# Column order of the inner MLP products: two halves of a row in turn, and other places for the rows

## The chip, the core and the metric

The kernel runs on one core of a Trainium2 chip. The metric is the time of one execution in microseconds (us), as the device reports it. A core has five instruction streams that matter here: PE (TensorE, matrix products; its weight loads are listed as PEld), DVE (VectorE), ACT (ScalarE), POOL (GpSimd) and SP, whose queue issues most of the DMAs. SBUF is the on-chip memory of 128 partitions that all engines read; PSUM takes the products.

## What is computed

One inference step of a decoder with two layers over 256 prompt tokens and 64 sample tokens, 320 columns in all, at width 2048. Layer 0 mixes tokens with gated linear attention, layer 1 with gMLP spatial gating. Each layer ends with a squared-ReLU MLP of inner width 8192 and two residual LayerNorms:

```
def sq_relu_mlp(x, w1, w2):
    return jnp.square(jax.nn.relu(x @ w1)) @ w2

x = layer_norm(DEEPNORM_ALPHA * x + h, ln1_g[i], ln1_b[i])
x = layer_norm(DEEPNORM_ALPHA * x + sq_relu_mlp(x, mlp_w1[i], mlp_w2[i]), ln2_g[i], ln2_b[i])
```

All inputs are float32. The change touches only the second MLP product, the one with w2.

## The kernel before

**Layout.** Activations lie transposed: features on the 128 partitions, the T = 320 tokens as columns. An activation of 2048 features is a tile of KT = 16 rows of 320 float32 per partition, 1280 bytes a row. `bigtile` allots BIG = 16 x 320 + 64 floats for it and begins the rows LINE // 2 = 32 floats (128 bytes) into the tile; `parts` makes two such tiles, a high and a low part. In the compiled program every one of these tiles begins at a multiple of 256 bytes, and a row is 5 x 256 bytes, so all rows of all high and low parts begin 128 bytes past a multiple of 256. The tile that feeds a fused LayerNorm (`dgh`, `dgl`) has rows of TW = 322 columns from offset 0: its row k begins 8k bytes past a multiple of 256.

**Products.** A float32 product is made of three products in the type float32r, each a matmul with 128 x 128 weights and 320 moving columns: low weights by high activations, high weights by low activations, high by high (`mm3`, lines 158 to 163). The three add into one PSUM bank. This document calls one such set a triple.

**Weights.** `unit` brings 512 rows by 256 columns of a weight matrix: one DMA of 512 KB from SP's queue, a cast on ACT for the high part `wh` (line 144), a subtraction on DVE for the low part `wl` (line 145). The parts lie in two rings of four buffers; each `wh` begins at a multiple of 256 bytes and each `wl` 64 bytes past one. `group` makes 256 output columns: four units, and for each unit two 128-column halves by four rows, that is 8 triples or 24 matmuls a unit. `gemm` runs eight groups.

**The MLP.** `mlp` works in four chunks of 2048 inner features. For chunk c, a gemm with w1 makes the chunk: its evictions (`evict`, `sq_relu`) square the ReLU and split it into `hh` (ACT, line 856) and `hl` (DVE, line 857). A gemm with w2 follows, with `hh` and `hl` as moving operands: 8 groups x 4 units x 24 = 768 matmuls, 256 triples. For chunks 0 to 2, `evz` adds each PSUM result to the residual `z` (DVE, line 876); for chunk 3, `residual_gemm` does so and feeds the LayerNorm. There are two layers, so eight such w2 stages; `h_in` names the tile pair, "b" in layer 0 and "a" in layer 1. The order of the instructions on an engine is the order of the calls here; `Side` objects spread other work between units, but none runs in the w2 stages.

Of the kernel before, what the change touches and what calls it, by code (L numbers as in the profile page):

```python
# [9 lines left out]
F32R = mybir.dt.float32r  # L10
# [6 lines left out]
D = 2048  # L17
KT = D // P
TP = 256
DB, DS = 8, 8  # L20
T = TP + DB * DS
# [10 lines left out]
UN = 256  # L32
NU = KT // UK
WARM = 9
LINE = 64
BIG = KT * T + LINE


# [6 lines left out]
class Ring:  # L45
# [5 lines left out]
    def part(self, p, name):  # L51

        t = self.pool.tile([P, UK, UN], F32R, tag=p + self.tag, name=name)
        if not self.gap:
            self.pool.tile([P, LINE // 4], F32, tag="gap", name=name + "_gap", bufs=1)
            self.gap = True
# [21 lines left out]
def step_kernel(ctx: ExitStack, tc: tile.TileContext, A):  # L78
# [3 lines left out]
    def nm(s):  # L82
        uid[0] += 1
        return f"{s}_{uid[0]}"
# [16 lines left out]
    def mmtile(n=T):  # L101

        if mx is not None:
            banks[0] = (banks[0] + 1) % 6
        return (mx if banks[0] > 3 else mm).tile([P, n], F32, tag="mm", name=nm("mm"), padded_shape=[P, 512])
# [16 lines left out]
    nc.vector.memset(eps_h[:], HEAD_EPS)  # L122
    cp.tile([P, LINE - 8], F32, tag="fill", name="fill")

# [4 lines left out]
    def unit(w, row0, q, col0, ring):  # L129

        raw = wraw.tile([P, UK, UN], F32, tag="raw", name=nm("raw"))
        src = w[row0 // (UK * P) + q, col0 // UN]
        hi = ring.part("h", nm("wh"))
        lo = ring.part("l", nm("wl"))
        units[0] += 1
        step = 2 if units[0] <= 2 else UK
        for k in range(0, UK, step):
            nc.sync.dma_start(raw[:, k : k + step, :], src[:, k : k + step, :])
        step = 1 if units[0] == 1 else step
        for k in range(0, UK, step):  # L140
            ks = slice(k, k + step)
            if units[0] == 1:
                before_unit(k)
            nc.scalar.copy(hi[:, ks, :], raw[:, ks, :])  # L144
            nc.vector.tensor_sub(lo[:, ks, :], raw[:, ks, :], hi[:, ks, :].bitcast(F32))  # L145
        return hi, lo
# [7 lines left out]
    def next_ring():  # L154
        turn[0] += 1
        return rings[turn[0] % len(rings)]

    def mm3(ps, wh, wl, kk, n, rh, rl, k, c0, cn, first, last):
        s = slice(n * P, (n + 1) * P)
        x_h, x_l = rh[:, k, c0 : c0 + cn], rl[:, k, c0 : c0 + cn]  # L160
        nc.tensor.matmul(ps, wl[:, kk, s], x_h, start=first, stop=False)  # L161
        nc.tensor.matmul(ps, wh[:, kk, s], x_l, start=False, stop=False)  # L162
        nc.tensor.matmul(ps, wh[:, kk, s], x_h, start=False, stop=last)  # L163

    def group(w, row0, cols, rh, rl, evict, side=None, width=T, before=None):

        ps = [mmtile(width) for _ in range(2 * len(cols))]
        for q in range(NU):
            if before is not None:
                before(q)  # L170
            for i, c in enumerate(cols):
                wh, wl = unit(w, row0, q, c, next_ring())
                for n in range(2):
                    for kk in range(UK):
                        k = q * UK + kk
                        mm3(ps[2 * i + n][:], wh, wl, kk, n, rh, rl, k, 0, width, k == 0, k == KT - 1)
                if side is not None:
                    side()
        for n in range(2 * len(cols)):
            evict(n, ps[n])  # L180
# [14 lines left out]
    w_in = A["gla_w_in"]  # L195
    C_Q, C_K, C_V, C_R = 0, H * DK, 2 * H * DK, 2 * H * DK + H * DV

    def bigtile(tag, dt, name, width=T):

        t = (lp if tag == "b1" else big).tile([P, BIG], dt, tag=tag, name=nm(name))
        start = LINE // 2 if width == T else 0
        return t[:, start : start + KT * width].rearrange("p (k t) -> p k t", t=width)

    def parts(pair, name, width=T):
        return bigtile(pair + "0", F32R, name + "h", width), bigtile(pair + "1", F32R, name + "l", width)

    xh, xl = parts("a", "x")  # L210
    o_all = bigtile("b0", F32, "o_all")
# [21 lines left out]
    def load_x(q):  # L233
        for i, raw in enumerate(x_in(q)):
            x_parts(slice(4 * q + 2 * i, 4 * q + 2 * i + 2), raw[:, :, 0:T])
# [55 lines left out]
    def load_gates():  # L291

        nc.sync.dma_start(wgr, A["gla_w_low"])
        wgr2 = gp.tile([P, 2, DV], F32, tag="vtp", name="wgr2")[:].rearrange("p a b -> p (a b)")
        for i in range(6):
            nc.sync.dma_start(wgr2[16 * i : 16 * (i + 1), :], A["gla_w_gate"])
        nc.scalar.copy(wg2[:], wgr2[0:96])
        nc.vector.tensor_sub(wg2[64:96, :], wgr2[64:96], wg2[64:96, :].bitcast(F32))
# [347 lines left out]
    for h, hd in enumerate(hds):  # L646
        gates = [hd.gate_logits, hd.gate_sums, hd.gate_decays]
        if h == 0:

            side = Side([lambda: None, lambda: load_x(1), lambda: None, lambda: load_x(2), lambda: load_gates(),  # L650
                         lambda: load_x(3), low_gate, *gates], 4 * NU)
# [5 lines left out]
        side = Side(hd.steps(), 2 * NU + (2 * NU if h < H - 1 else 2))  # L657
# [10 lines left out]
    def second_half():  # L668
# [12 lines left out]
        rings.append(Ring(wb, "b"))  # L681
        wb.tile([P, LINE // 4], F32, tag="fill", name="fill_b", bufs=1)
        z = lp.tile([P, KT, T], F32, tag="z", name="z")
        lp.tile([P, 3 * LINE // 4], F32, tag="fill", name="fill_l")
        for q in range(2):
# [112 lines left out]
            nc.vector.tensor_mul(t[:], t[:], self.rstd[:])  # L798
            return t, wgb[:, 1:2]

    def gemm(w, row0, col0, rh, rl, evict, quad=False, side=None, before=None, before_last=None):

        i = 0
        while i < D // UN:
            n2 = 2 if quad and i == 0 else 1
            group(w, row0, [col0 + (i + m) * UN for m in range(n2)], rh, rl,
                  lambda n, ps, i=i: evict(2 * i + n, ps), side, before=before if i == 0 else before_last if i == D // UN - 1 else None)
            i += n2

    def gemm_of(norm, out, w, col0, evict_raw, evict):  # L810
# [7 lines left out]
            group(w, 0, (col0 + i * UN,), yh, yl, lambda n, ps, i=i: evict(2 * i + n, ps))  # L818
        return yh, yl

    def residual_gemm(w, rh, rl, row0, scale, vg, vb, raw, quad=False, side=None, before=None, last=False):

        norm = None

        def evict(j, ps):
            nonlocal norm
            if j == 0:
                norm = Norm(z, vg, vb, raw, last)
            zj = z[:, j, :]
            if j < KT // 2:  # L830
                nc.vector.scalar_tensor_tensor(zj, zj, scale, ps[:], op0=ALU.mult, op1=ALU.add)
            else:
                nc.vector.tensor_add(zj, zj, ps[:])
            norm.add(j)
            if j == KT // 2 - 1:
                for i in range(KT // 2, KT):
                    zi = z[:, i, :]
                    nc.vector.scalar_tensor_tensor(zi, zi, scale, norm.c[:], op0=ALU.mult, op1=ALU.subtract)

        gemm(w, row0, 0, rh, rl, evict, quad, side, before)  # L840
        return norm

    def mlp(i, norm, y_in, h_in, vg, vb, raw, last=False):

        w1, w2 = A["mlp_w1"][i], A["mlp_w2"][i]
        NC_ = 4
        for c in range(NC_):
            hs = []

            def sq_relu(j, x, r):  # L850
                if not hs:
                    hs.extend(parts(h_in, "h"))
                hh, hl = hs
                f = l2.tile([P, T], F32, tag="f", name=nm("f"))
                nc.vector.scalar_tensor_tensor(f[:], x, 0.0, r[:], op0=ALU.max, op1=ALU.mult)
                nc.scalar.copy(hh[:, j, 0:T], f[:])  # L856
                nc.vector.tensor_sub(hl[:, j, 0:T], f[:], hh[:, j, 0:T].bitcast(F32))  # L857

            def evict(j, ps):
                r = l2.tile([P, T], F32, tag="r", name=nm("r"))  # L860
                nc.scalar.activation(r[:], ps[:], AF.Relu)
                sq_relu(j, ps[:], r)

            def evict_raw(j, ps):
                t, wb_ = norm.correct(ps)
                r = l2.tile([P, T], F32, tag="r", name=nm("r"))
                nc.scalar.activation(r[:], t[:], AF.Relu, bias=wb_)
                sq_relu(j, r[:], r)

            if c == 0:  # L870
                yh, yl = gemm_of(norm, y_in, w1, 0, evict_raw, evict)
            else:
                gemm(w1, 0, c * D, yh, yl, evict)
            if c < NC_ - 1:
                def evz(j, ps, s=ALPHA if c == 0 else 1.0):
                    nc.vector.scalar_tensor_tensor(z[:, j, :], z[:, j, :], s, ps[:], op0=ALU.mult, op1=ALU.add)
                gemm(w2, c * D, 0, *hs, evz)
            else:
                return residual_gemm(w2, *hs, c * D, 1.0, vg, vb, raw, last=last)


    def before(q):
        if q == NU - 1:
            second_half()
        else:
            split_o(range(UK * q, UK * (q + 1)))

    norm = residual_gemm(A["gla_w_out"], oh, ol, 0, ALPHA, V_L1G, V_L1B, "b", quad=True,
                         side=side, before=before)
# [87 lines left out]
    side = Side(steps, 6 * NU)  # L977
# [23 lines left out]
    ps = {}  # L1001
# [103 lines left out]
```

## Time and profile before

| what | value |
|---|---|
| median of 3 runs | 2704.8 us (2704.26 to 2705.38) |
| profiled execution, its own time | 2703.75 us |
| span of the profiled execution | 2702.0 us |
| instructions on PE | 18515 matmuls, 18515 weight loads |
| read from HBM | 409.60 MB |

The span runs from the first to the last instruction of the profile; the execution's own time lies 1.75 us above it. [...]

The eight w2 stages lie as follows (first matmul with `hh` or `hl`, us from the span's start; layer 0, then layer 1): 667.1, 889.0, 1110.9, 1332.7; 1907.0, 2128.8, 2350.7, 2572.6. Each is about 110.9 us long. Between them lie the w1 gemms of the same length.

### The profile page before, as it was taken

The numbers are of one execution on the slowest core, as the hardware profiler recorded it, in microseconds if no ns is written. First come the engines' busy times: TensorE is split into PE (matmuls) and PEld (weight loads), VectorE is DVE, ScalarE is ACT, GpSimd is POOL, SyncE is SP. The second block draws the span as 40 slices with busy tenths as digits, with TensorE's granted clock in tenths as the row PEclk, the third lists the DMA queues.
The fourth block names the chain that finished last, engine by engine and source line by source line (L and its number), as shares of the span: only waits on it lengthen the run. The fifth ranks groups of instructions, "written<-read, shape, count | busy, mean of one in ns | idle before, by whom it ended". The sixth has DMA issues, their size and how long they took to land.

```text
span 2702.0 us, 44679 instructions
## 1 busy us (share of the span) xinstructions
PE 2692.4 (100%) x18515; PEld 2669.7 (99%) x18515; DVE 1543.5 (57%) x2289; ACT 1182.8 (44%) x1702; POOL 53.5 (2%) x83
## 2 busy tenths in 40 slices
PE   9999999999999999999999999999999999999998
PEld 9999999999999999999999999999999999999998
DVE  6667577885444444444468775587444444444456
ACT  6545455464234334333445554355334323333434
POOL 1000001000000000000001000000000000000000
PEclk9999999999999999999999999999999999999999
DMA  7656556644445455444445444454444545554442
GB/s 243 193 188 228 185 190 218 211 146 156 152 151 154 151 154 151 153 151 153 150 148 171 150 140 136 140 162 155 150 155 150 154 151 153 152 153 152 153 152 79
DMA packets 126396, 434.53 MB, mean 161 GB/s; under 512 B 13680, under 2 KB 17904, under 8 KB 126192
## 3 DMA queue, kind: packets, MB, share of 16 engines
q1 hardware_dynamic: 119136, 407.82, 48.6%
q0 software_dynamic: 6512, 23.20, 2.6%
q8 instruction: 145, 2.38, 0.4%
q10 hardware_dynamic: 544, 0.66, 0.1%
q14 instruction: 59, 0.48, 0.1%
HBM read 409.60 MB, written 22.02 MB: 160 GB/s over the span
## 4 chain that ended last, share of the span: by engine, by line
PE 99%; ACT 0%; DMA 0%; DVE 0%; issue 0%; ACTq 0%; DVEq 0%
PE mm L161 32%; PE mm L163 31%; PE mm L162 31%; PE gl L600 1%; PE gl L603 1%; PE gl L558 1%; PE gl L948 0%; PE gl L542 0%; DMA raw<-gla_w_in 0%; ACT z L1038 0%; PE gl L943 0%; DMA xr<-xT 0%; PE gl L543 0%; PE gl L458 0%; PE gl L456 0%; PE gl L521 0%
## 5 line engine op out<-in xcount | busy, mean ns | idle before, releaser
L145 DVE TENSOR_TENSOR wl<-raw,wh 128x1024 fp32r<-128x1024 f32 (+1 forms) x740 | 901.6, 1219 | 938.8 <-ACT wh L144 936.3
L144 ACT CAST wh<-raw 128x1024 fp32r<-128x1024 f32 (+1 forms) x740 | 771.3, 1044 | 1201.3 <-PE mm L163 1080.9
L163 PE MATMUL mm<-yh,wh 128*128 128x320 f32 x2624 | 805.0, 307 | 0.0
L161 PE MATMUL mm<-yh,wl 128*128 128x320 f32 x2624 | 803.1, 308 | 0.0
L162 PE MATMUL mm<-yl,wh 128*128 128x320 f32 x2624 | 794.2, 303 | 0.0
L161 PE MATMUL mm<-hh,wl 128*128 128x320 f32 x2048 | 630.8, 308 | 0.0
L163 PE MATMUL mm<-hh,wh 128*128 128x320 f32 x2048 | 628.7, 307 | 0.0
L162 PE MATMUL mm<-hl,wh 128*128 128x320 f32 x2048 | 619.6, 303 | 0.0
L162 PEld LDWEIGHTS mm<-yl,wh 128*128 128x128 f32 x2624 | 492.5, 188 | 0.0
L161 PEld LDWEIGHTS mm<-yh,wl 128*128 128x128 f32 x2624 | 490.9, 188 | 0.0
L163 PEld LDWEIGHTS mm<-yh,wh 128*128 128x128 f32 x2624 | 490.8, 187 | 0.0
L162 PEld LDWEIGHTS mm<-hl,wh 128*128 128x128 f32 x2048 | 384.4, 188 | 0.0
L161 PEld LDWEIGHTS mm<-hh,wl 128*128 128x128 f32 x2048 | 384.4, 188 | 0.0
L163 PEld LDWEIGHTS mm<-hh,wh 128*128 128x128 f32 x2048 | 383.0, 187 | 0.0
L161 PE MATMUL mm<-xh,wl 128*128 128x320 f32 x768 | 241.1, 314 | 0.9 <-DVE wl L145 0.5
L163 PE MATMUL mm<-xh,wh 128*128 128x320 f32 x768 | 236.7, 308 | 0.0
L162 PE MATMUL mm<-xl,wh 128*128 128x320 f32 x768 | 234.7, 306 | 0.0
L161 PEld LDWEIGHTS mm<-xh,wl 128*128 128x128 f32 x768 | 144.1, 188 | 5.4 <-issue 1.9
L162 PEld LDWEIGHTS mm<-xl,wh 128*128 128x128 f32 x768 | 144.3, 188 | 3.5 <-issue 1.2
L163 PEld LDWEIGHTS mm<-xh,wh 128*128 128x128 f32 x768 | 143.9, 187 | 1.3
L857 DVE TENSOR_TENSOR hl<-f,hh 128x320 fp32r<-128x320 f32 x128 | 62.3, 489 | 29.4 <-ACT hh L856 29.4
L161 PE MATMUL mm<-oh,wl 128*128 128x320 f32 x256 | 78.1, 309 | 0.6 <-DVE nw L187 0.6
(268 smaller groups left out, 2112.2 us busy)
## 6 DMA issues: line engine op xcount, KB each, us to landing
raw<-mlp_w SPq DMA_DIRECT2D x512, 512.0 KB, 3.5
raw<-gla_w_in SPq DMA_DIRECT2D x94, 512.0 KB, 4.2
raw<-sg_w_in SPq DMA_DIRECT2D x64, 512.0 KB, 3.5
st<-state SPq DMA_DIRECT2D x32, 512.0 KB, 4.3
o_state_s<-st POOLq DMA_DIRECT2D x32, 512.0 KB, 3.8
raw<-gla_w_out SPq DMA_DIRECT2D x32, 512.0 KB, 4.2
raw<-sg_w_out SPq DMA_DIRECT2D x32, 512.0 KB, 3.5
z<-xT POOLq DMA_DIRECT2D x2, 1280.0 KB, 11.6
```

The costliest lines, as they stand in the source:

```text
L144: nc.scalar.copy(hi[:, ks, :], raw[:, ks, :])
L145: nc.vector.tensor_sub(lo[:, ks, :], raw[:, ks, :], hi[:, ks, :].bitcast(F32))
L161: nc.tensor.matmul(ps, wl[:, kk, s], x_h, start=first, stop=False)
L162: nc.tensor.matmul(ps, wh[:, kk, s], x_l, start=False, stop=False)
L163: nc.tensor.matmul(ps, wh[:, kk, s], x_h, start=False, stop=last)
L558: nc.tensor.matmul(pu[:], hd.ktp[:, blk, kt * P : (kt + 1) * P], hd.vtp[:, blk, :], start=(blk == 0), stop=(blk == 1))
L600: nc.tensor.matmul(po[:], qm[:, kt, b * P : (b + 1) * P], part[:], start=False, stop=(b == DB - 1 and kt == 1 and part is sth))
L603: nc.tensor.matmul(pu[:], kz[:, g, i, kt * P : (kt + 1) * P], hd.vts[:, g, :], start=True, stop=True)
L857: nc.vector.tensor_sub(hl[:, j, 0:T], f[:], hh[:, j, 0:T].bitcast(F32))
```

## The change

A table `TURNS` gives every w2 stage two numbers: the offset in floats at which the rows of `hh` and `hl` begin in their tiles, and a run length. With a run length, `by_turns` views the 320 columns of a matmul's moving operand and of its PSUM output as two halves of 160, and orders them as a run from the first half, the run at the same place of the second half, the next run of the first, and so on. The same columns meet the same PSUM addresses as before; only the order in which they pass is another. Chunk 0 of layer 0 keeps its offset and its plain order.

| stage | layer 0, c=0 | c=1 | c=2 | c=3 | layer 1, c=0 | c=1 | c=2 | c=3 |
|---|---|---|---|---|---|---|---|---|
| offset, floats | 32 | 32 | 32 | 32 | 16 | 0 | 48 | 16 |
| run, floats | none | 4 | 8 | 16 | 4 | 4 | 4 | 8 |

The other lines of the diff pass the two numbers down through `gemm`, `residual_gemm`, `group`, `parts` and `bigtile`.

```
+TURNS = [[(32, None), (32, 4), (32, 8), (32, 16)], [(16, 4), (0, 4), (48, 4), (16, 8)]]
...
-    def mm3(ps, wh, wl, kk, n, rh, rl, k, c0, cn, first, last):
+    def by_turns(ap, run):
+
+        return ap if run is None else ap.rearrange("p (j i e) -> p i j e", j=2, e=run)
+
+    def mm3(ps, wh, wl, kk, n, rh, rl, k, c0, cn, first, last, run):
         s = slice(n * P, (n + 1) * P)
-        x_h, x_l = rh[:, k, c0 : c0 + cn], rl[:, k, c0 : c0 + cn]
+        ps, x_h, x_l = (by_turns(ap, run) for ap in (ps, rh[:, k, c0 : c0 + cn], rl[:, k, c0 : c0 + cn]))
         nc.tensor.matmul(ps, wl[:, kk, s], x_h, start=first, stop=False)
         nc.tensor.matmul(ps, wh[:, kk, s], x_l, start=False, stop=False)
         nc.tensor.matmul(ps, wh[:, kk, s], x_h, start=False, stop=last)
...
-    def bigtile(tag, dt, name, width=T):
+    def bigtile(tag, dt, name, width=T, start=None):
...
-        start = LINE // 2 if width == T else 0
+        start = start if start is not None else LINE // 2 if width == T else 0
...
-                    hs.extend(parts(h_in, "h"))
+                    hs.extend(parts(h_in, "h", start=TURNS[i][c][0]))
...
-                gemm(w2, c * D, 0, *hs, evz)
+                gemm(w2, c * D, 0, *hs, evz, run=TURNS[i][c][1])
             else:
-                return residual_gemm(w2, *hs, c * D, 1.0, vg, vb, raw, last=last)
+                return residual_gemm(w2, *hs, c * D, 1.0, vg, vb, raw, last=last, run=TURNS[i][c][1])
```

More of the change, by code (lines that the diff above doesn't have):

```diff
@@ L163, in mm3, with group @@
         nc.tensor.matmul(ps, wh[:, kk, s], x_h, start=False, stop=last)
-    def group(w, row0, cols, rh, rl, evict, side=None, width=T, before=None):
+    def group(w, row0, cols, rh, rl, evict, side=None, width=T, before=None, run=None):
         ps = [mmtile(width) for _ in range(2 * len(cols))]
@@ L175, in group @@
                         k = q * UK + kk
-                        mm3(ps[2 * i + n][:], wh, wl, kk, n, rh, rl, k, 0, width, k == 0, k == KT - 1)
+                        mm3(ps[2 * i + n][:], wh, wl, kk, n, rh, rl, k, 0, width, k == 0, k == KT - 1, run)
                 if side is not None:
@@ L196, in step_kernel, with parts @@
     C_Q, C_K, C_V, C_R = 0, H * DK, 2 * H * DK, 2 * H * DK + H * DV
-    def bigtile(tag, dt, name, width=T):
+    def bigtile(tag, dt, name, width=T, start=None):
         t = (lp if tag == "b1" else big).tile([P, BIG], dt, tag=tag, name=nm(name))
-        start = LINE // 2 if width == T else 0
+        start = start if start is not None else LINE // 2 if width == T else 0
         return t[:, start : start + KT * width].rearrange("p (k t) -> p k t", t=width)
-    def parts(pair, name, width=T):
-        return bigtile(pair + "0", F32R, name + "h", width), bigtile(pair + "1", F32R, name + "l", width)
+    def parts(pair, name, width=T, start=None):
+        return (bigtile(pair + "0", F32R, name + "h", width, start),
+                bigtile(pair + "1", F32R, name + "l", width, start))
     xh, xl = parts("a", "x")
@@ L799, in correct, with gemm @@
             return t, wgb[:, 1:2]
-    def gemm(w, row0, col0, rh, rl, evict, quad=False, side=None, before=None, before_last=None):
+    def gemm(w, row0, col0, rh, rl, evict, quad=False, side=None, before=None, before_last=None, run=None):
         i = 0
@@ L806, in gemm @@
             group(w, row0, [col0 + (i + m) * UN for m in range(n2)], rh, rl,
-                  lambda n, ps, i=i: evict(2 * i + n, ps), side, before=before if i == 0 else before_last if i == D // UN - 1 else None)
+                  lambda n, ps, i=i: evict(2 * i + n, ps), side, before=before if i == 0 else before_last if i == D // UN - 1 else None,
+                  run=run)
             i += n2
@@ L819, in gemm_of, with residual_gemm @@
         return yh, yl
-    def residual_gemm(w, rh, rl, row0, scale, vg, vb, raw, quad=False, side=None, before=None, last=False):
+    def residual_gemm(w, rh, rl, row0, scale, vg, vb, raw, quad=False, side=None, before=None, last=False, run=None):
         norm = None
@@ L838, in evict @@
                     nc.vector.scalar_tensor_tensor(zi, zi, scale, norm.c[:], op0=ALU.mult, op1=ALU.subtract)
-        gemm(w, row0, 0, rh, rl, evict, quad, side, before)
+        gemm(w, row0, 0, rh, rl, evict, quad, side, before, run=run)
         return norm
```

## The prediction

> **What bounds the kernel now.** I read the page's busy shares, clock row and chain first, then the windows, then single matmuls.
>
> ```profile
> span 2702.0 us, 44679 instructions
> PE 2692.4 (100%) x18515; PEld 2669.7 (99%) x18515; DVE 1543.5 (57%) x2289; ACT 1182.8 (44%) x1702; POOL 53.5 (2%) x83
> PEclk9999999999999999999999999999999999999999
> PE 99%; ACT 0%; DMA 0%; DVE 0%; issue 0%; ACTq 0%; DVEq 0%
> PE mm L161 32%; PE mm L163 31%; PE mm L162 31%; PE gl L600 1%; PE gl L603 1%; PE gl L558 1%; PE gl L948 0%; PE gl L542 0%; DMA raw<-gla_w_in 0%; ACT z L1038 0%; PE gl L943 0%; DMA xr<-xT 0%; PE gl L543 0%; PE gl L458 0%; PE gl L456 0%; PE gl L521 0%
> ```
>
> The chain of work that ended last is PE for 99%, and 94% are the three lines of the triple. The clock is full in all 40 slices. So the time is the pace of these matmuls, and nothing that frees DVE, ACT or the DMAs is worth anything by itself. The windows show the stages concerned (columns: stretch, its length, then each engine's busy time and rows).
>
> ```profile
> core 0: us, PE busy (x) PEld busy (x) DVE busy (x) ACT busy (x) POOL busy (x), PEclk, DMA share, GB/s
> 889.00:999.90 110.90, 110.90 (x770) 110.90 (x769) 47.21 (x50) 34.24 (x34) 0.00 (x0) 1.00 0.50 152
> ...
> 1794.60:1823.40 28.80, 28.80 (x197) 28.80 (x196) 24.46 (x45) 20.33 (x37) 0.00 (x0) 1.00 0.50 147
> ```
>
> The first is one w2 stage: 768 matmuls in 110.9 us, 144.4 ns each, 433.3 ns a triple. PE never pauses; so what can change is the distance between matmuls. The timeline of that stage (start, duration) shows that it isn't the same for the three products:
>
> ```profile
> 900.12 0.31 PE L163 MATMUL mm<-hh,wh 128*128 128x320 f32 x1
> 900.26 0.31 PE L161 MATMUL mm<-hh,wl 128*128 128x320 f32 x1
> 900.41 0.30 PE L162 MATMUL mm<-hl,wh 128*128 128x320 f32 x1
> 900.55 0.31 PE L163 MATMUL mm<-hh,wh 128*128 128x320 f32 x1
> 900.70 0.31 PE L161 MATMUL mm<-hh,wl 128*128 128x320 f32 x1
> 900.85 0.30 PE L162 MATMUL mm<-hl,wh 128*128 128x320 f32 x1
> 900.99 0.31 PE L163 MATMUL mm<-hh,wh 128*128 128x320 f32 x1
> 901.13 0.31 PE L161 MATMUL mm<-hh,wl 128*128 128x320 f32 x1
> 901.28 0.30 PE L162 MATMUL mm<-hl,wh 128*128 128x320 f32 x1
> 901.42 0.31 PE L163 MATMUL mm<-hh,wh 128*128 128x320 f32 x1
> ```
>
> From 900.12 to 901.42 are three triples, 1.30 us or 433.3 ns each. L162 holds the stream for 0.14 us, L161 for 0.15, L163 for 0.14 or 0.15. In nanoseconds, means over the 256 triples of which these rows are a part: L161 147.5, L162 140.0, L163 145.8. All three move 320 columns, and the rows of `hh` and `hl` begin at the same place modulo 256 bytes; L161 and L162 even load the same next weights. So 140.0 is no count of columns that all must pay: on 320 columns two of three products lose 6 to 7.5 ns. What loses them?
>
> ```profile
> L162 PE MATMUL mm<-hl,wh x2048: 302/303/311, 667.3 to 2684.0; 128*128 128x320 f32 x187
> ...
> L162 PE MATMUL mm<-dgl,wh x192: 303/309/314, 555.0 to 1823.3; 128*128 128x322 f32 x192
> ```
>
> These are the shortest, middle and longest duration of two groups. `hl` rows all begin at one place modulo 256 and nearly all take 303. `dgl` rows shift by 8 bytes from row to row, and spread over 303 to 314, with a middle of 309. DVE and ACT can't be the cause, since they work for 47.2 and 34.2 of 110.9 us, in bursts, while the 303 stays. I conclude that the loss comes from within PE's two reads: the columns now moving and the weights of the next product are read from SBUF at once, and where they meet depends on the places they start from.
>
> [...]
>
> **The change part by part.** *Instructions:* none is added or removed; a matmul is still one row with 320 columns, and each DMA, cast and eviction stands where it stood. In PSUM each column keeps its address, so `evz` and the LayerNorm read as before. *Offsets:* the ACT cast and DVE subtraction that write `hh` and `hl` write to other addresses, 16 of each a w1 stage; if that cost anything it would be covered:
>
> ```profile
> L144 ACT CAST wh<-raw 128x1024 fp32r<-128x1024 f32 x32 | 33.5, 1048 | 74.2 <-PE mm L163 74.2
> L145 DVE TENSOR_TENSOR wl<-raw,wh 128x1024 fp32r<-128x1024 f32 x32 | 39.2, 1225 | 57.6 <-ACT wh L144 57.6
> ```
>
> (columns: busy us, mean ns, idle before and who ended it). ACT sits idle 74.2 us of the stage until PE gives back a weight buffer. I price it at nothing; were the cover gone it would show as PE idle. *What is late next if PE gets faster:* a unit feeds 24 matmuls, 3.47 us at 144.4 ns and 3.36 at 140. Of its makers ACT takes 1.05 and DVE 1.23 us, and 512 KB in 3.36 us are 156 GB/s.
>
> ```profile
> GB/s 243 193 188 228 185 190 218 211 146 156 152 151 154 151 154 151 153 151 153 150 148 171 150 140 136 140 162 155 150 155 150 154 151 153 152 153 152 153 152 79
> ```
>
> The DMAs moved 243 GB/s in the first slice, so the 152 now is the consumer's pace, and 156 is no limit. Any gain or loss of the matmuls goes to the end in full.
>
> *Column order and place:* this is the only term. Seven stages of 256 triples, 1792 triples, 776.5 us. No row of before shows an order by turns, so I bound it. Below: L161 and L163 lose 7.5 and 5.8 ns against 140.0; all at 140 is 420.0 a triple, 13.3 less, 23.9 us over seven stages. Whether 140 itself holds such a loss no row shows; the outer bound takes as much again as the mean loss from all three products: 140 - 6.65 = 133.3, 400 a triple, 59.7 us less. Above: the `dg` stage, whose rows start anywhere from 0 to 120 bytes. Its 197 rows include about two at the edges that start outside; 28.8 us by 195 is 147.7 ns for mostly 322 columns. Two columns at 140/320 = 0.44 ns off: 146.8, or 440.5 a triple, 7.2 more, 12.9 us. A price for turning has no upper row of its own (third rival).
>
> Within the bounds I take a value for each run length. In the plain order 320 columns pass while 128 weights are read: the moving read goes 2.5 times as far as the other and keeps overtaking it. By turns, each half advances only 160 columns in that time, 1.25 times the weights' way. Once pushed clear of each other, such reads stay clear for longer. I value this as the best product of the trace, three times 140.0, for run 4, where the halves advance nearly together: 4 stages x 256 x 13.3 ns = 13.6 us. For run 8, where each half waits twice as long for its turn, half of it: 2 x 256 x 6.65 = 3.4 us. For run 16, which over a whole turn resembles the plain order, nothing. I make no difference between offsets 0, 16, 32 and 48. Sum: 17.0 us. From the profiled execution, 2703.75 us (span 2702.0 and 1.75 around it), that gives 2686.7; its time lies 1.05 below the median of the runs, 2704.8, so the forecast for the median is **2688**.
>
> **The rivals.** *First, no change.* [...] For it: PE's total hardly differs between stages (110.9 us each). [...] It gives 2705, and covers mixed outcomes that cancel among seven settings.
>
> *Second, slower by place.* The halves lie 640 bytes apart, that is 2.5 x 256: an order by turns reads at two opposite places modulo 256, and four stages move the rows too. If the present place is merely the best one, the pace falls to that of the `dg` rows, 440.5 a triple. Price 7.2 ns x 1792 = 12.9 us: 2718. It decides where a stage's mean goes above 144.4 ns; 111.5 us for a stage is already its side. For it: the present place beats the mean of the others in the trace. Against: the `dg` rows shift from row to row, so they never stay in a good relation, while here every row begins alike.
>
> *Third, slower by turning.* If each jump costs one column's time, 0.44 ns (140/320), a product with run 4 has 80 jumps, 35 ns; run 8 17.5, run 16 8.75: 4 x 768 x 35 + 2 x 768 x 17.5 + 768 x 8.75 ns = 141 us, 2846. Above 0.05 ns a jump it outweighs my gain. No row shows a jump, for or against. [...]
>
> **How the numbers follow.** Forecast and its neighbours below no change: 0.48. First rival 0.20, second 0.20, third 0.12. Likeliest is the forecast, 2688. The range takes in the first and second rivals, to 2724 for a dearer place than the mean, and below goes two thirds of the way to the outer bound: 17.0 + 0.55 x (59.7 - 17.0) is 40 us, 2664. Left out are the third rival and about 0.07 below. By signs, with 0.2% (5.4 us, about what a measurement can tell from no change): faster 0.48, same 0.20, slower 0.32. The likeliest case alone lies between 2664 and 2699.
>
> **What would show it.** The windows of the seven stages: 107.5 us where run is 4, about 109.2 at run 8, 110.9 at run 16 and in the unchanged stage at 667. L161 and L163 should take 303 like L162. The first rival shows 110.9 everywhere; the second 112.8 and durations near 309; the third stage lengths in the order of the run: 4 the longest, 137.8 us, 16 nearest to 110.9. If offsets 0, 16, 48 differ widely at the same run, I was wrong to treat them as one. I am wrong altogether if turns cost something, or if PE idles before a matmul in these stages.

## The result, and the profile after

The changed kernel takes 2746.6 us (median of 4 runs, 2746.4 to 2747.0) against 2704.7 before: a ratio of 1.0155, 95% interval 1.0137 to 1.0172. It is 41.9 us slower; the forecast was 2688, the range ended at 2724. The profiled execution took 2746.37 us, with a span of 2744.7, 42.7 us more than before. The page after, the rows that answer to those of before:

```profile
span 2744.7 us, 44680 instructions
PE 2735.5 (100%) x18515; PEld 2712.4 (99%) x18515; DVE 1543.3 (56%) x2289; ACT 1183.4 (43%) x1702; POOL 53.8 (2%) x83
PEclk9999999999999999999999999999999999999999
PE 99%; ACT 0%; DMA 0%; DVE 0%; issue 0%; ACTq 0%
L168 PE MATMUL mm<-yl,wh 128*128 128x320 f32 x2624 | 794.3, 303 | 0.0
L167 PE MATMUL mm<-hh,wl 128*128 128x320 f32 x2048 | 646.4, 316 | 0.0
L168 PE MATMUL mm<-hl,wh 128*128 128x320 f32 x2048 | 645.9, 315 | 0.0
L169 PE MATMUL mm<-hh,wh 128*128 128x320 f32 x2048 | 645.2, 315 | 0.0
```

PE still makes 99% of the chain, with the same 18515 matmuls at full clock (1.00 in every window below) and 2.2 us of waits in all (2.6 before), none of them in these stages; DVE and ACT work as long as before (1543.5 and 1182.8). What grew are the matmuls of `hh` and `hl` alone: means of 315 and 316 ns where 303 to 308 stood, over all eight stages, the unchanged one included. Those of `yl` stay at 303. The rows of `hh` and `hl` before:

```profile
L161 PE MATMUL mm<-hh,wl 128*128 128x320 f32 x2048 | 630.8, 308 | 0.0
L163 PE MATMUL mm<-hh,wh 128*128 128x320 f32 x2048 | 628.7, 307 | 0.0
L162 PE MATMUL mm<-hl,wh 128*128 128x320 f32 x2048 | 619.6, 303 | 0.0
```

The windows of six stages after (stretch, length, busy time and rows of each engine) say where:

```profile
667.60:778.50 110.90, 110.90 (x769) 110.90 (x769) 47.19 (x50) 34.24 (x34) 0.00 (x0) 1.00 0.48 152
889.40:1007.20 117.80, 117.80 (x771) 117.80 (x769) 47.23 (x50) 34.69 (x35) 0.00 (x0) 1.00 0.45 144
1118.10:1234.10 116.00, 116.00 (x770) 116.00 (x769) 47.19 (x50) 34.27 (x35) 0.00 (x0) 1.00 0.46 146
1345.10:1461.20 116.10, 116.10 (x771) 116.10 (x770) 73.96 (x116) 47.31 (x69) 0.00 (x0) 1.00 0.47 146
1924.50:2042.30 117.80, 117.80 (x771) 117.80 (x770) 47.20 (x50) 34.70 (x34) 0.00 (x0) 1.00 0.46 143
2153.20:2271.00 117.80, 117.80 (x771) 117.80 (x770) 47.20 (x50) 34.36 (x34) 0.00 (x0) 1.00 0.46 144
```

The unchanged stage keeps 110.9 us. The same 256 triples take 117.8 us with run 4 (460.0 ns a triple) and 116.0 with runs 8 and 16 (453.3). Run 4 gives 460.0 at offset 32 as at 16 and 0, and at 48 too (117.7). So four stages lose 26.7 ns on 256 triples, 27.3 us, and three about 20.0 ns, 15.4 us: the whole difference of 42.7. The timeline of one run-4 stage (`hh` and `hl` at offset 16; start, duration) shows that no product is spared:

```profile
1930.01 0.32 PE L167 MATMUL mm<-hh,wl 128*128 128x320 f32 x1
1930.17 0.32 PE L168 MATMUL mm<-hl,wh 128*128 128x320 f32 x1
1930.32 0.32 PE L169 MATMUL mm<-hh,wh 128*128 128x320 f32 x1
1930.47 0.32 PE L167 MATMUL mm<-hh,wl 128*128 128x320 f32 x1
```

The rows overlap: each lasts 0.32 us, and they start about 0.15 us apart. What a matmul costs the stream is read as the distance from its start to the next one's. That makes 0.46 us for three, against 0.433 before; the high-by-low product that took 140 ns now takes 154.

Below, "a triple" is a stage's mean distance between starts, summed over the three products; its length in us is that times 0.256.

### The profile page after: what moved, and what is told of

Read it like the earlier page. It is cut to its first block, busy times and chain, and to the rows that moved or that the text cites. A ratio compares the mean times of both kernels' runs of the same rounds, so it can differ in the third digit from the quotient of the medians.

```text
span 2744.7 us, 44680 instructions
## 1 busy us (share of the span) xinstructions
PE 2735.5 (100%) x18515; PEld 2712.4 (99%) x18515; DVE 1543.3 (56%) x2289; ACT 1183.4 (43%) x1702; POOL 53.8 (2%) x83
## 4 chain that ended last, share of the span: by engine, by line
PE 99%; ACT 0%; DMA 0%; DVE 0%; issue 0%; ACTq 0%
PE mm L167 32%; PE mm L169 31%; PE mm L168 31%; PE gl L607 1%; PE gl L610 1%; PE gl L565 1%; PE gl L956 0%; PE gl L549 0%; DMA raw<-gla_w_in 0%; ACT z L1046 0%; PE gl L951 0%; DMA xr<-xT 0%; PE gl L550 0%; PE gl L465 0%; PE gl L463 0%; PE gl L528 0%
## 5 line engine op out<-in xcount | busy, mean ns | idle before, releaser
L167 PE MATMUL mm<-hh,wl 128*128 128x320 f32 x2048 | 646.4, 316 | 0.0
L168 PE MATMUL mm<-hl,wh 128*128 128x320 f32 x2048 | 645.9, 315 | 0.0
L169 PE MATMUL mm<-hh,wh 128*128 128x320 f32 x2048 | 645.2, 315 | 0.0
```

## The experiments

Each w2 stage can be given its own setting, so that most kernels measure six to eight settings. All start from the changed kernel, with offsets and block counts put into the table: an entry is the offset of `hh`, that of `hl`, then the order of the moving columns and of the PSUM columns as (blocks, run), None for plain. Most of these kernels were run once; the stages left plain at offset 32 in them serve as controls, and with the weights whole and in their place they took 433.3 ns each time.

### Order, place, and which side

**Places alone.** `TURNS` all plain, other offsets:

```
+TURNS = [[(32, 32, None, None), (16, 16, None, None), (0, 0, None, None), (48, 48, None, None)],
+         [(32, 0, None, None), (32, 16, None, None), (32, 48, None, None), (0, 32, None, None)]]
```

> All eight w2 stages in plain column order; only the places differ (offsets of hh and hl in floats: layer 0 32/32, 16/16, 0/0, 48/48; layer 1 32/0, 32/16, 32/48, 0/32). In the changed kernel every stage with run 4 took 460.0 ns a triple, at four different places. If the moved rows carry the loss, the stages at 16, 0 and 48 take 450 to 460 here too. If the order carries it, they take 433 to 446 (what the dg rows spread over), the control at 32/32 433.3. If reads meet by place, the four stages with unequal places differ among themselves by 5 ns a triple or more; if place is nothing without turns, all eight stages show 433.3, 110.9 us.

That execution took 6703 us. Its matmuls of `y`, which no edit touches, lay mostly about 275 or 403 ns apart, while a weight cast on ACT took 1041 ns and a subtraction on DVE 1219 (1044 and 1219 before). Its page has no `PEclk` row, so it does not tell whether PE's clock was lowered; nothing is drawn from it. The same kernel again:

> The same kernel as e1_places: plain order in all w2 stages, offsets of hh and hl 32/32, 16/16, 0/0, 48/48 in layer 0 and 32/0, 32/16, 32/48, 0/32 in layer 1. In that first run every stage, also those that no edit touches, was 2 to 2.6 times as long, so nothing could be read from it. If the moved rows carry part of the changed kernel's loss, the stages at 16, 0 and 48 take over 440 ns a triple; if place without turns is worth nothing, all eight take 433.3.

It took 2714.1 us. The first four stages:

```profile
667.60:778.50 110.90, 110.90 (x770) 110.90 (x769) 47.21 (x50) 34.24 (x34) 0.00 (x0) 1.00 0.48 152
889.50:1001.00 111.50, 111.50 (x770) 111.50 (x770) 47.18 (x50) 34.27 (x34) 0.00 (x0) 1.00 0.48 152
1111.90:1224.50 112.60, 112.60 (x770) 112.60 (x769) 47.19 (x50) 34.27 (x34) 0.00 (x0) 1.00 0.47 150
1335.50:1448.30 112.80, 112.80 (x772) 112.80 (x771) 73.89 (x116) 47.44 (x68) 0.00 (x0) 1.00 0.47 150
```

433.3 ns a triple at offset 32, 435.5 at 16, 440.0 at 0 and 48; with unequal offsets 440.0, 436.7, 440.0 and 441.3. In plain order the place counts, by 2 to 8 ns. The changed kernel's stages at these places lose 27, and as much as the one that stayed at 32: the moved rows are not its cause.

**Runs and blocks.**

```
+TURNS = [[(32, 32, (2, 2), (2, 2)), (32, 32, (2, 32), (2, 32)), (32, 32, (2, 80), (2, 80)), (32, 32, (2, 160), (2, 160))],
+         [(32, 32, (5, 4), (5, 4)), (32, 32, (5, 8), (5, 8)), (32, 32, (5, 16), (5, 16)), (32, 32, (5, 32), (5, 32))]]
```

> All rows at offset 32. Layer 0: two halves by turns with runs 2, 32, 80 and 160 (160 is the plain order written as a three-dimensional pattern). Layer 1: five blocks of 64 columns by turns, 256 bytes apart, with runs 4, 8, 16, 32. If each jump costs by itself, the loss over 433.3 ns a triple follows the number of jumps: run 2 the largest, above 460; run 32 and 80 small; five blocks at run 4 as two halves at run 4, 460. If two reads meet in SBUF, the loss does not follow the count: five blocks, which all lie at one place modulo 256 bytes, differ from two halves at the same run by 5 ns or more. If the pattern's form costs, run 160 is above 433.3; otherwise it is 433.3.

Two halves: run 2 617.2, run 32 443.3, run 80 446.7, run 160 433.3. Five blocks: 511.1, 461.9, 446.6, 453.3 for runs 4 to 32. The form of the pattern is free: run 160, the plain order in that form, takes 433.3 as well. The loss is no price per jump: run 80 has 3 jumps a matmul and loses 13.3 ns a triple, run 32 has 9 and loses 10.0, run 16 19 and 20.0, run 4 79 and 26.7. And the same run from five blocks is another matter. The windows of run 32, run 80 and five blocks with run 4:

```profile
936.10:1049.60 113.50, 113.50 (x771) 113.50 (x770) 47.22 (x50) 34.19 (x34) 0.00 (x0) 1.00 0.47 149
1160.50:1274.80 114.30, 114.30 (x770) 114.30 (x769) 47.21 (x50) 34.25 (x35) 0.00 (x0) 1.00 0.48 148
...
1960.10:2090.90 130.80, 130.80 (x769) 130.80 (x769) 47.18 (x50) 35.20 (x34) 0.00 (x0) 1.00 0.41 129
```

**One side.** The moving columns by turns with PSUM plain in layer 0, the other way round in layer 1:

```
+TURNS = [[(32, 32, (2, 4), None), (32, 32, (2, 8), None), (32, 32, (2, 16), None), (32, 32, None, None)],
+         [(32, 32, None, (2, 4)), (32, 32, None, (2, 8)), (32, 32, None, (2, 16)), (32, 32, None, None)]]
```

> Turns on one side only, at offset 32: layer 0 chunks 0 to 2 move the columns by turns (runs 4, 8, 16) and write PSUM in plain order; layer 1 chunks 0 to 2 move them in plain order and write PSUM by turns (runs 4, 8, 16). Chunk 3 is plain in both layers. The step that puts the columns back in order is left out. If the loss is in the SBUF read, layer 0 shows 460, 453 and 453 ns a triple and layer 1 433.3 in all; if it is in the PSUM write, the other way round; if both share it, both lie between.

The windows of the runs 4 and 8, first by turns when read, then when written:

```profile
667.00:784.70 117.70, 117.70 (x769) 117.70 (x768) 47.19 (x50) 34.68 (x34) 0.00 (x0) 1.00 0.46 144
895.70:1011.70 116.00, 116.00 (x769) 116.00 (x769) 47.17 (x50) 34.25 (x34) 0.00 (x0) 1.00 0.47 146
1923.90:2034.80 110.90, 110.90 (x770) 110.90 (x769) 47.21 (x50) 34.26 (x34) 0.00 (x0) 1.00 0.48 152
2145.80:2256.70 110.90, 110.90 (x770) 110.90 (x770) 47.19 (x50) 34.26 (x34) 0.00 (x0) 1.00 0.48 152
```

460.0, 453.3 and 453.3 against 433.3 three times: for these runs the whole loss is on the side of the moving columns, none in the PSUM write.

### Do the weights take part?

**Fewer weight columns** (only that many output rows are made):

```
-        s = slice(n * P, (n + 1) * P)
+        s = slice(n * P, n * P + wc)
...
+        ps = by_turns(ps[0:wc], out)
```

> Fewer weight columns, at offset 32: layer 0 plain order, run 4 and run 8 with 64 of 128 columns; layer 1 plain and run 4 with 32 columns, run 16 with 64. Chunk 3 is full and plain in both layers. The other output rows of these products are left out. If the loss comes from reading the next weights beside the moving columns, it shrinks with them: over 400 ns a triple, plain 33 to about 17, run 4 60 to about 30, with 32 columns to 8 and 15. If jumps cost by themselves, run 4 stays 26.7 ns above plain at 64 and at 32 columns. If the loss is a fixed price of a weight load, all stay at 433, 460 and 453.

Plain with 64 columns, two halves run 4 with 64, then run 4 with 32:

```profile
667.10:778.90 111.80, 111.80 (x770) 103.36 (x769) 47.05 (x50) 34.25 (x34) 0.00 (x0) 1.00 0.51 151
889.80:1007.50 117.70, 117.70 (x770) 104.79 (x768) 47.08 (x50) 34.80 (x34) 0.00 (x0) 1.00 0.46 144
...
2143.30:2261.00 117.70, 117.70 (x770) 86.30 (x768) 47.01 (x50) 34.14 (x35) 0.00 (x0) 1.00 0.45 144
```

The weight loads did get shorter: PEld's busy time (the second pair) falls to 104.8 and 86.3 us. Run 4 stays at 460.0 with 128, 64 and 32 columns, runs 8 and 16 with 64 columns at 453.3. Plain even rises, 433.3, 436.7, 440.0. My theory expected run 4 to fall to about 430 and 415, counted from 400, the prediction's outer bound and an estimate. What the two halves show would also fit a price paid once for each weight load, whatever its length; plain, which moves, does not.

**Fewer weight columns with other blocks** (the same edit; 64 columns in layer 0, 32 in layer 1):

> Offset 32, run 4 from four, sixteen and five blocks, with 64 weight columns in layer 0 and 32 in layer 1; chunk 3 is full, in layer 0 four blocks, in layer 1 plain. The other output rows of these products are left out. With 128 columns these took 420.0, 500.0 and 511 ns a triple. If the moving read loses against itself alone, all six stay within 2 ns of that, as two halves stayed at 460.0. If the weights' read takes part where pieces lie at other distances, sixteen and five blocks fall by 10 ns or more with fewer weights.

Sixteen blocks 500.0 in both, five blocks 511.7 and 508.2, four blocks 426.7 and 420.0. Nothing falls by 10 ns, but not all stay within 2 ns either: four blocks with 64 columns rise by 6.7, five with 32 fall by 2.9.

**The weights at another place.** Each low part begins 64 bytes past a multiple of 256; here it begins at one, like the high part:

```
-            self.pool.tile([P, LINE // 4], F32, tag="gap", name=name + "_gap", bufs=1)
+            self.pool.tile([P, 64], F32, tag="gap", name=name + "_gap", bufs=1)
```

A second filler behind the ring keeps all other tiles where they were, modulo 256.

> Low weights at the place of the high ones, offset 32; layer 0: two halves with runs 4, 8 and 16, then plain; layer 1: five, sixteen and four blocks with run 4, then plain. Before this move they took 460.0, 453.3, 453.3, 433.3 and 511, 500, 420.0, 433.3 ns a triple. Plain is known to go to 440.0 and four blocks to 420.0. If the predicted meeting with the weights has any part in the halves' loss, runs 4, 8 and 16 move by 6.7 ns or more; if the loss of halves is the moving read's alone, they stay at 460 and 453, and five and sixteen blocks at 511 and 500 within 2 ns.

Two halves: 460.0 and 453.3 for runs 4 and 16, as before; run 8 went from 453.3 to 459.9. Five blocks 510.0, sixteen 500.0, four 424.4, plain 440.0. The windows of runs 4 and 8:

```profile
673.50:791.20 117.70, 117.70 (x769) 117.70 (x768) 47.15 (x50) 34.19 (x34) 0.00 (x0) 1.00 0.45 144
903.90:1021.60 117.70, 117.70 (x770) 117.70 (x768) 47.16 (x50) 34.16 (x34) 0.00 (x0) 1.00 0.46 144
```

So the loss of two halves at run 4 is there (460.0) with every amount of weights and at both places of the low ones that were tried. Neither forecast holds whole: at run 8 the place of the weights is worth 6.6 ns. Over these orders it moves a triple by up to 6.7 ns, far less than the 20 to 27 that two halves lose.

**The order of the products**, plain:

```
+        three = ((wl[:, kk, s], x_h), (wh[:, kk, s], x_l), (wh[:, kk, s], x_h))
+        for m in range(3):
+            lhs, rhs = three[order[m]]
+            nc.tensor.matmul(ps, lhs, rhs, start=first and m == 0, stop=last and m == 2)
```

> Plain order of columns, the three products of a triple in another order (0 is low weights by high, 1 high by low, 2 high by high): layer 0: 0-2-1, 1-0-2, 1-2-0, 2-0-1; layer 1: 2-1-0, then hl at offset 0 with 0-2-1 and with 0-1-2, then hl at offset 48 with 0-1-2. If the 140.0 ns of the high-by-low product belongs to its own two operands, the triple stays 433.3 in every order at 32/32 and the 140.0 goes with it. If it belongs to the pair of weights (the next product loads the same ones), it goes to whichever product stands ahead of a second load of wh. If it belongs to the sequence, totals differ; 420 or less in any of them would be a version faster than both kernels.

433.3 in all five orders at 32/32. The 140.0 ns goes to the product whose own weights and whose successor's are both high parts: high by high in the orders 0-2-1, 1-0-2 and 2-1-0, high by low in 1-2-0 and 2-0-1. `hl` at 0 or 48 gave 440.0. So in plain order the 140.0 ns goes with the weights around a product, not with its own moving columns. That the two weights begin at one place is not the reason: with the low ones moved to the place of the high ones (the last run of this section), no product keeps 140.

### Which distances

**Eight ways to cut a row**, mostly with run 4, as (blocks, run): (4, 4), (8, 4), (10, 4), (16, 4), then (20, 4), (40, 4), (4, 8), (80, 2).

> Runs of 4 columns from 4, 8, 10, 16 blocks in turn in layer 0 and from 20 and 40 blocks in layer 1, so that pieces that follow each other lie 320, 160, 128, 80, 64 and 32 bytes apart; then 4 blocks with run 8, and 80 blocks of 4 columns with run 2. Offset 32. Two halves (640 bytes apart) gave 460.0 and five blocks (256 bytes apart) 511 ns a triple, with 80 pieces each. If the number of pieces sets the loss, all six run-4 stages show about 460. If the moving read is slowed by meeting itself at the same place modulo some power of two, distances of 64 and 32 bytes, or 128, come out far apart: by over 20 ns. If only neighbouring 16-byte pieces are fast, all are above 460. The last stage reads each 16 bytes in two visits: like run 2 of two halves, 617, if a visit costs; 440 or less if a visit close to the last is free.

```profile
667.00:774.50 107.50, 107.50 (x770) 107.50 (x769) 47.20 (x50) 34.20 (x34) 0.00 (x0) 1.00 0.50 157
885.50:1003.20 117.70, 117.70 (x769) 117.70 (x769) 47.19 (x50) 34.23 (x34) 0.00 (x0) 1.00 0.45 144
1114.20:1231.90 117.70, 117.70 (x770) 117.70 (x769) 47.19 (x50) 34.35 (x34) 0.00 (x0) 1.00 0.45 144
1342.90:1471.00 128.10, 128.10 (x770) 128.10 (x770) 74.02 (x116) 47.89 (x68) 0.00 (x0) 1.00 0.43 132
1934.20:2044.70 110.50, 110.50 (x771) 110.50 (x770) 47.17 (x50) 34.25 (x34) 0.00 (x0) 1.00 0.49 153
2155.60:2268.20 112.60, 112.60 (x770) 112.60 (x769) 47.19 (x50) 34.20 (x34) 0.00 (x0) 1.00 0.48 150
...
2601.10:2821.80 220.70, 220.70 (x774) 159.85 (x774) 66.68 (x109) 40.24 (x61) 0.00 (x0) 1.00 0.17 55
```

Four blocks take 107.5 us, 420.0 ns a triple: what I had forecast for two, and the fastest stage so far. Eight and ten blocks 460.0, sixteen 500.0, twenty 431.6, forty 440.0; four with run 8 433.4. Pieces of 4 columns number 80 in each of the first six, so their number decides nothing. The last stage visits each 16 bytes twice, two columns at a time: 860 ns. Visits of two float32r columns take 860 ns a triple here (617.2 from two halves), visits of four in the same neighbourhood 440.0 (forty blocks). Whether that is the read's doing is not shown: PSUM was written by twos as well, and the test of each side covers runs of 4, 8 and 16 only.

**Four blocks at other offsets, longer runs.** Offsets 16, 0, 48 and 32/0 with (4, 4); then (4, 16), (4, 20), (4, 40), (20, 8) at 32.

> Four blocks with run 4 at offsets 16, 0 and 48, then hh at 32 with hl at 0; in layer 1 at offset 32 four blocks with runs 16, 20 and 40, then 20 blocks with run 8. Run 4 at offset 32 gave 420.0 ns a triple, run 8 433.4; 20 blocks with run 4 gave 431.6. If the distance between successive pieces decides alone, all four stages of layer 0 show 420.0; if the starting place counts as it does in plain order (433.3 to 440 there), they spread by 2 to 7 ns. If the gain needs a new distance at every 16 bytes, runs 16, 20 and 40 show 433 or more, as two halves did (453, and 447 at run 80).

426.7, 426.7, 430.0, 426.8: all below plain at 32 (433.3), and 7 to 10 ns above the 420.0 of four blocks at 32, so the place counts here too. Longer runs: 440.0, 460.0, 440.0, and 437.3 for (20, 8). Only runs of 4 gained.

**Other widths**, full weights, the other columns not made:

```
+        mv, out, wc, cn = run or (None, None, P, cn)
...
+        ps = by_turns(ps[0:wc, 0:cn], out)
```

> Fewer moving columns with all 128 weight columns, to make other distances between blocks, run 4, offset 32. Layer 0: 288 columns plain, two halves (576 bytes apart), three blocks (384 bytes); layer 1: 288 columns from six blocks (192 bytes), 256 columns from two halves (512 bytes), 256 columns plain; chunk 3 is full and plain. The other columns of these products are left out. If the remainder of the distance modulo 256 decides, two halves of 288 (remainder 64, as 320 bytes) come out at or below plain of 288 columns, three blocks (128, as 640 bytes) 20 ns a triple or more above it, two halves of 256 (0, as 256 bytes) 50 or more above plain of 256. If two halves as such are slow, both of them stand 20 to 30 above their plain order. If only nearness counts, 576 is as bad as 640.

288 columns: plain 393.4, two halves 413.3, three blocks 406.6, six 385.1. 256 columns: plain 360.0, two halves 386.7. The rule by remainders fell: two halves 576 bytes apart (remainder 64, like the good 320) lose 20. Two halves lose 20 to 27 ns at 512, 576 and 640 bytes.

**Fewer columns with 32 weight columns**, by the same edit:

> Fewer moving columns with 32 weight columns; layer 0: 240 columns plain, run 4, run 8; layer 1: 160 columns plain, run 4, run 8; chunk 3 full and plain in both. The other output rows and columns of these products are left out. With 32 weight columns, 320 columns plain took 440.0 and run 4 460.0 ns a triple. At 133.3 ns for 320 columns, plain pays 13.3 ns a matmul above the columns themselves, run 4 20.0. If plain's part is paid once a matmul, 240 columns take 113.3 each, 340 a triple, and 160 take 240. If it is paid per column, 330 and 220. If the turns' part is per piece, run 4 stands 15 ns a triple above plain at 240 columns and 10 at 160; if once a matmul, 20 at both.

240 columns: plain 320.1, run 4 343.8, run 8 340.0. 160 columns: plain 221.4, runs 4 and 8 230.0. The plain stage of 160 columns still lasts as long as the others: near and at its end PE waits four times for weights, 3 us in all, which its 221.4 leaves out. Before that its matmuls pass faster, as the count of rows in equal stretches of the three stages (plain, run 4, run 8) shows:

```profile
1831.00:1866.00 35.00, 35.00 (x478) 35.00 (x476) 20.93 (x25) 16.45 (x17) 0.00 (x0) 1.00 0.69 225
2002.00:2037.00 35.00, 35.00 (x459) 35.00 (x458) 21.15 (x26) 17.44 (x18) 0.00 (x0) 1.00 0.72 227
2173.00:2208.00 35.00, 35.00 (x460) 35.00 (x458) 21.67 (x25) 17.62 (x18) 0.00 (x0) 1.00 0.71 231
```

Neither forecast holds at both widths: plain was to take 340 and 240 by one, 330 and 220 by the other. The 133.3 ns from which the first was counted is the prediction's outer bound (140 - 6.65), an estimate that no run shows: the fastest stage of 320 columns took 420.0, 140.0 a product. Two more distances for two halves come out of it: 480 bytes, 23.7 ns a triple lost, and 320 bytes, 8.6. Four blocks of 80 columns lie 320 bytes apart as well and gain, also with 32 weight columns (420.0 against 440.0): the distance alone does not decide.

### Versions

**Four blocks for two, the rest of the change kept:**

```
-        return ap if run is None else ap.rearrange("p (j i e) -> p i j e", j=2, e=run)
+        return ap if run is None else ap.rearrange("p (j i e) -> p i j e", j=4, e=run)
```

> The changed kernel with one number altered: four blocks of 80 in place of two halves of 160; its offsets and its runs of 4, 8 and 16 are kept. If the distance of 640 bytes makes the changed kernel's loss, and neither turning as such nor the moved rows, the four run-4 stages go from 460 to about 420 ns a triple and the run-8 stages from 453 to about 433: the kernel is faster than the one before by about 4 x 256 x 13.3 ns = 14 us, 2691 us, against 2746.6. If the moved rows count as in plain order, up to 7 us of that are lost. If turning costs, it stays above 2720.

2699.6 us, 0.9983 of before (0.9974 to 0.9993): the change's sign turns with one digit, though the gain is only 4 us, below the 7 to 14 expected. Its run-4 stages take 420.0, 426.7, 426.7 and 430.0, run 8 433.4 and 440.0, run 16 440.0.

**Four blocks, run 4, in every product of 320 columns:**

```
-        ps, x_h, x_l = (by_turns(ap, run) for ap in (ps, rh[:, k, c0 : c0 + cn], rl[:, k, c0 : c0 + cn]))
+        mv, out = run or (((4, 4), (4, 4)) if cn == T else (None, None))
+        x_h, x_l = (by_turns(ap, mv) for ap in (rh[:, k, c0 : c0 + cn], rl[:, k, c0 : c0 + cn]))
+        ps = by_turns(ps, out)
```

> All products of 320 columns in the whole kernel take their columns from four blocks of 80, four columns at a time, all rows at offset 32. One w2 stage did so at 420.0 ns a triple against 433.3. If that belongs to the distance of 320 bytes and holds for every pair of tiles, the 5696 triples of 320 columns gain 13.3 ns each, 76 us: about 2629 us, with stages of 107.4 us instead of 110.9. If it was peculiar to that stage's tiles, the stages with y, x and o stay at 433.3 or above and the gain is about 2048 x 13.3 ns = 27 us or less: 2677 us or more.

2658.8 us, 0.9833 of before (0.9819 to 0.9848), between the two forecasts. Most stages run at 426.7, not 420.0, and the last groups of two stages at 420 with the same addresses. The stage with `hh` and `hl` at 32 that gave 420.0 when it alone had four blocks gives 426.7 here, with the same instructions and addresses. What differs is what ran before it, so that sets which of two steady paces it keeps.

**The same with the low weights moved.** First to the place of the high ones (the edit above), then 128 bytes past it (32 floats of gap):

> As e8_four_everywhere, but the low weights begin at the same place modulo 256 bytes as the high ones (64 bytes apart before). There most stages ran at 426.7 ns a triple and some at 420.0 with the same addresses. If the weights' places set which pace is taken, it moves: all at 420.0 (2622 us), or all at another multiple of 6.7 above. If the moving read sets it alone, stages stay at 426.7 and 420.0 as before, 2659 us.

> As e8_four_everywhere, with the low weights 128 bytes past the place of the high ones, which is the place of the moving rows. Same reading: a pace other than 426.7 in the stages shows that the weights' places take part; 420.0 everywhere would be 2622 us; no change 2659 us.

At the place of the high ones: 2635.6 us, 0.9746 of before (0.9732 to 0.9761). The timeline of one stage has one pace for all three products:

```profile
899.71 0.30 PE L172 MATMUL mm<-hh,wl 128*128 128x320 f32 x1
899.85 0.30 PE L173 MATMUL mm<-hl,wh 128*128 128x320 f32 x1
899.99 0.30 PE L174 MATMUL mm<-hh,wh 128*128 128x320 f32 x1
900.13 0.30 PE L172 MATMUL mm<-hh,wl 128*128 128x320 f32 x1
900.27 0.30 PE L173 MATMUL mm<-hl,wh 128*128 128x320 f32 x1
```

140 ns each, 420.0 a triple in six of the eight stages; the two that feed a LayerNorm begin at 420.0 and end at 424.4. 128 bytes past: 2675.3 us (0.9892, 0.9876 to 0.9909), about 428.9. The moved weights alone, in plain order:

> The kernel before with plain order everywhere, and the low weights at the place of the high ones modulo 256 bytes. In plain order the 140.0 ns always fell to the product whose own weights and whose successor's weights begin at the same place, whichever operands it had (e7). If that pairing is the reason, all three products now take 140.0, 420 ns a triple, about 2629 us. If weights at one constant place give the pace of the gate product that has such (146.7 ns), it is 440 a triple, about 2743 us. If the weights' place is nothing, 433.3 and 2704 us.

2739.1 us, 440.0 in every stage, each product at 146 to 147 ns. So two weights at one place do not give 140, as one forecast had it; the 440 of the other came true. The same move gains 23 us beside four blocks and costs 35 beside plain order.

## Why the prediction was wrong

- **What bounds the kernel: right.** The path is PE's pace throughout, and the 42.7 us lie in the seven stages. No cover was needed: added instructions none, DVE and ACT as before (1543.3 and 1183.4 us), PSUM order free (433.3 written by turns).
- **The failing step** is in the part on column order and place: "Once pushed clear of each other, such reads stay clear for longer", valued at three times 140.0 for run 4. It rests on the conclusion that the loss comes from PE's two reads, moving columns and next weights, meeting. The rows show that the weight load for the next product starts with each matmul (one at 900.12 us beside the L163 at 900.12), not that either waits for the other; that such reads push each other clear was my assumption, which no run shows. For two halves at run 4 such a meeting by place is refuted: with a half and a quarter of the weight columns, with the low weights moved, and with the moving rows at four offsets, the triple stays at 460.0. In place of the 13.3 ns gained, a triple loses 26.7 at run 4 and 20.0 at runs 8 and 16; and it is lost on the side of the moving columns, not in the PSUM write. At run 8 the place of the weights adds a step of 6.6 ns.
- **Where the conclusion came from.** The rows of before showed that the pace depends on places; the weights were one explanation, and for plain order they do take part: moving them shifts it from 433.3 to 440.0. How they do so no run shows. I let a cause that fits a step of 7 ns carry a forecast for another order, without a row of that order.
- **No difference by offset: right for two halves at run 4** (460.0 at four offsets), by luck: the prediction gave no reason for it. In plain order it is 2 to 8 ns.
- **Second rival, slower by place:** the sign was right, the price of 7.2 ns too small by a factor of about three, and its reason wrong: offsets change nothing for two halves at run 4, and a distance with another remainder (576 bytes) loses 19.9 ns as well.
- **Third rival, slower by turning:** its sign was right, and run 4 is the longest stage as it said. It was wrong as a price per jump; 80 pieces cost from 78 ns a triple (five blocks) to a gain of 13 (four). Its number, 2846, was far off. **First rival:** no stage kept 110.9 but the unchanged one.
- **The range** ended at 2724 because its upper side took the spread of plain orders (`dg` rows) as the bound for an order no row showed. The far bound, left out with 0.12, was the side on which the time lay.

Open: why two halves lose at every distance tried while four blocks gain. Neither the count of pieces nor the distance nor its remainder orders the results; no run tells what in the read does. No run did without the weight loads, so a price paid once a load, whatever its length and place, is not excluded for two halves. Nor is it shown how what ran before picks between the paces 420.0 and 426.7.

## What to carry to other kernels

Where PE never waits and its matmuls still differ by a few per cent at the same shape, the order in which moving columns are read is a term of its own, worth from -3% to +18% of a stage's time here with runs of 4 columns or more, and has to be measured. Give each stage of one kernel its own setting and read the stages, not the total: one run then measures eight settings, and the sum of good and bad ones (the changed kernel) tells little. Then measure the chosen one in the whole kernel: the 420.0 of four blocks alone became 426.7 with four blocks everywhere. Test order and weight placement together; the placement that cost 35 us in plain order gained 23 us with four blocks.

## What the runs showed of the hardware that was not expected

- Many steady paces lie on steps: 420.0, 426.7, 433.3, 440.0, 453.3, 460.0, 500.0 ns a triple are all multiples of 6.67, and most such stages keep one over 256 triples. Others do not (428.9, 435.5, 511.1). Two paces can belong to the same addresses, depending on what ran before.
- PSUM takes its columns by turns of 4, 8 or 16 from two halves at no cost (433.3 in all three).
- Fewer weight columns hardly make a stream of 320 columns faster: with a quarter of them plain order went from 433.3 to 440.0, two halves at run 4 stayed at 460.0, and the most gained was 2.9 ns a triple (five blocks).
- In one execution PE's matmuls alone ran about 2 to 2.6 times as far apart (6703 us), with ACT's casts and DVE's subtractions as long as before (1041 and 1219 ns) and no clock row in its profile; the same kernel then took 2714.
